# A state times its queries: one full-precision matmul becomes three passes over split operands

## The chip, the cores and the metric

The kernel runs on one core of a Trainium2 chip. The metric is the device time of one execution in microseconds. The engines named below: TensorE (PE, with its weight loads PEld), VectorE (DVE), ScalarE (ACT), GpSimd (POOL), and SyncE (SP), whose queue issues the DMAs.

## The reference, cut to what matters

The program is one layer of an encoder: a projection of 2048 tokens, a gated linear recurrence in both directions (8 heads of 128), a neighbourhood attention (16 heads of 64), a gate on each, an output projection and a norm. The change lies in the recurrence. One direction of it, chunk by chunk:

```python
def step(state, xs):
    qc, kc, vc, dc = xs
    o = jnp.einsum('bhtd,bhdv->bhtv', qc, state)
    state = dc[..., None] * state + jnp.einsum('bhtd,bhtv->bhdv', kc, vc)
    return state, o
...
o = direction(zf_fw, lb_fw, False) + direction(zf_bw, lb_bw, True)
o = _rmsnorm(o.transpose(0, 2, 1, 3), norm_g).reshape(B, S, HG_WIDTH)
return o.astype(g_in.dtype) * jax.nn.silu(g_in)
```

The backward direction runs over the tokens from the last to the first. So an output of the first 1024 tokens needs the backward state that the last 1024 tokens leave.

## The kernel before, in words

All work is in float32. Where a product may not lose precision, an operand is split in a high part that fits a shorter format (float32r) and the low rest, and the product is made as three matmuls: high x high, high x low, low x high. The projections (`proj_mm`, line L278, and `vproj`, line L291) are made so. Other products take plain float32 operands in one call, L676 among them; the profile shows such a call as two records.

The recurrence (`hgrn`, `hgrn_tail`) goes over the 8 heads with the first 1024 tokens (first half, `half == 0`), and then over the 8 heads with the last 1024 (second half). A half has two groups of 512 tokens (`g`), a group four blocks of 128. In the first half the backward state that will come in from the second half isn't known yet. So `hgrn_tail` stores for each head and group, in DRAM:

- `op_d`: the output as far as it is known (tile `ob`);
- `sg_d`: the gate;
- `qb_d`: the queries, decayed to the end of the half (tile `qb`, made on VectorE at L663).

In the second half, when the head's backward state `R` (tiles of the tag `Sb`, L647 and L649) is complete, `hgrn_tail` loads these three again (L671 to L673, tiles of the tag `cl`, a ring of three buffers), multiplies `R` with the queries (L676), adds the stored output (L677), and goes through the norm (`rms_out`: the square at L345, its split at L347 and L349, two matmuls with ones at L354 and L355, ScalarE at L357 and L358, VectorE at L359 and L361, the store to `yq` at L362).

`weave` mixes two streams on TensorE: the steps of the recurrence, and the projection for the next head (L278), whose weights come through `load_split` (loads L262 into a ring of four, split on ScalarE at L268 and on VectorE at L269). The tail of one head (`hgrn_tail`) runs inside the next head's steps. TensorE's order is the order in which the code emits; the other engines' and SP's order is set by a scheduler that places each instruction by a simulated time and by priority. Where the recurrence ends and the attention begins, the two phases share memory and are ordered as one list, TensorE's rows too.

The attention's second half begins with copies: `Prep.k` copies keys into `KA` and `KB` on ScalarE (L978), then copies each to the other 64 partitions by DMA (L979), three pieces each; `load_bias` (L732) loads two bias tables; `alone` fills `Z` (L766); the first score matmuls are L1041 and L1046. The last values for the attention are projected meanwhile by `vproj` (L291), emptied from PSUM on ScalarE (L299, tile `vt`) and stored to `nv` (L301).

Two numberings are used: line numbers are those of the kernel before; in the changed kernel everything from L677 on stands eight lines later.

Of the kernel before, what the change touches and what calls it, by code (L numbers as in the profile page):

```python
# [10 lines left out]
F32 = mybir.dt.float32  # L11
F32R = mybir.dt.float32r
U32 = mybir.dt.uint32
AF = mybir.ActivationFunctionType
ALU = mybir.AluOpType
# [4 lines left out]
P = 128  # L20
KT = D // P
HALF = 1024
GRP = 512
NHEAD = 8
# [14 lines left out]
def body(ctx: ExitStack, tc: tile.TileContext, t):  # L39
    nc = tc.nc  # L40
    dve, act, pool, pe = nc.vector, nc.scalar, nc.gpsimd, nc.tensor
    dma = nc.sync.dma_start
    x, out = t["x"], t["out"]
# [9 lines left out]
    @contextmanager  # L53
    def psum_phase(name, psb, pmap={}):
        with tc.tile_pool(name="p" + name, bufs=1, space=PSUM, reuse_waits="tile") as q:
            cur.update(psum=q, ps=psb, map=pmap)
            yield

    @contextmanager
    def phase(name, bufs, smap={}):  # L60
        with tc.tile_pool(name=name, bufs=1, reuse_waits="tile") as p:
            cur.update(pool=p, bufs=bufs, smap=smap)
            yield

    def dram(name, shape, dt=F32):
        if name in t:
            return t[name]
        return nc.dram_tensor(name, shape, dt, kind="Internal").ap()
# [4 lines left out]
    c_d = dram("c_d", (D,))  # L73
    hs = [dram(f"hs{k}", (P, 2, HALF)) for k in range(KT)]
    op_d = [dram(f"op{i}", (P, HALF)) for i in range(NHEAD)]
    qb_d = [dram(f"qb{i}", (P, HALF)) for i in range(NHEAD)]
    sg_d = [dram(f"sgd{i}", (P, HALF)) for i in range(NHEAD)]
    nq_d = [dram(f"nq{i}", (P, 512)) for i in range(NPAIR)]
    nk_d = [dram(f"nk{i}", (P, 768)) for i in range(NPAIR)]
# [8 lines left out]
    def nm(s):  # L88
        cnt[0] += 1
        return f"{s}_{cnt[0]}"  # L90

    def tl(tag, dt=F32, shape=None):
        if tag in cur["smap"]:
            tag = cur["smap"][tag]
            return sh.tile([P, 512], dt, tag=tag, name=nm(tag), bufs=SH[tag])
        return cur["pool"].tile([P, 512] if shape is None else shape, dt, tag=tag, name=nm(tag), bufs=cur["bufs"].get(tag, 1))
# [4 lines left out]
    def ps(tag="mx"):  # L101
        if tag == "pj":
            return pp.tile([P, 512], F32, tag=tag, name=nm("pj"))
        tag = cur["map"].get(tag, tag)
        return cur["psum"].tile([P, 512], F32, tag=tag, name=nm("ps"), bufs=cur["ps"][tag])
# [221 lines left out]
    def hgrn_init():  # L327
        p = cur["pool"]
        msk["mskd"] = p.tile([P, 3, 32], F32, tag="mskd", name="mskd")
        dma(msk["mskd"], t["mskd"])  # L330
        for i in range(2):
            b = p.tile([P, 2 * P], F32, tag=f"pdb{i}", name=f"pdb{i}")
            pool.memset(b, 0.0)
            pdb.append(b)
        for u in range(NHEAD):
            sfb.append(p.tile([P, P], F32, tag=f"sfb{u}", name=f"sfb{u}"))
# [6 lines left out]
    def rms_out(u, g, o_sb, sg, tok, rest=False):  # L343
        sq = tl("t")
        act.activation(sq, o_sb, AF.Square)  # L345
        sh_ = tl("rh", F32R)
        dve.tensor_copy(sh_, sq)  # L347
        sl_ = tl("rl", F32R)
        dve.tensor_tensor(sl_, sq, sh_, op=ALU.subtract)  # L349
        yield  # L350
        if rest:
            yield
        pss = ps("ss")
        pe.matmul(pss, ones, sh_, start=True, stop=False)  # L354
        pe.matmul(pss, ones, sl_, start=False, stop=True)  # L355
        r = tl("t")
        act.activation(r, pss, AF.Ln, scale=1.0 / 128.0, bias=eps_rms)  # L357
        act.activation(r, r, AF.Exp, scale=-0.5)  # L358
        dve.tensor_mul(r, r, o_sb)  # L359
        yv = tl("t")  # L360
        dve.tensor_tensor(yv, r, sg, op=ALU.mult)  # L361
        dma(yT[u][:, tok:tok + 512], yv)  # L362
# [60 lines left out]
    def hgrn(u, half, st, tail):  # L423
# [197 lines left out]
        for _ in tail:  # L621
            pass
        return hgrn_tail(u, half, sgs, ubs, decs, qibs, os_, decb_all)

    HSUM = 54

    def hgrn_tail(u, half, sgs, ubs, decs, qibs, os_, decb_all):

        R = None
        if half == 0:  # L630
            ds_ = tl("dsuf", shape=[P, 8])
            pool.memset(ds_[:, 7:8], 1.0)
            for b in range(6, -1, -1):
                dve.tensor_mul(ds_[:, b:b + 1], ds_[:, b + 1:b + 2], decb_all[:, b + 1:b + 2])
        obs = {}
        for g in (1, 0):
            po = os_[g]
            pend = []
            for b in range(3, -1, -1):
                sl = slice(b * P, (b + 1) * P)  # L640
                if R is not None:
                    pend.append((sl, R))
                if half == 0 and g == 0 and b == 0:
                    break
                rn = tl("Sb", shape=[P, P])
                if R is None:
                    dve.tensor_copy(rn, ubs[g][:, sl])  # L647
                else:
                    dve.scalar_tensor_tensor(rn, R, decs[1, g][:, b:b + 1], ubs[g][:, sl], op0=ALU.mult, op1=ALU.add)  # L649
                R = rn  # L650
            yield
            for sl, r in pend:
                pe.matmul(po[:, sl], r, qibs[1, g][:, sl], start=False, stop=True, skip_group_check=True)
            ob = tl("t")
            act.activation(ob, po, AF.Copy)
            tk = slice(g * 512, (g + 1) * 512)
            if half == 0:
                dma(op_d[u][:, tk], ob)
                dma(sg_d[u][:, tk], sgs[g])
                qb = tl("t")  # L660
                for b in range(4):
                    sl = slice(b * P, (b + 1) * P)
                    dve.tensor_scalar(qb[:, sl], qibs[1, g][:, sl], ds_[:, g * 4 + b:g * 4 + b + 1], 1.0, op0=ALU.mult, op1=ALU.mult)  # L663
                dma(qb_d[u][:, tk], qb)
            else:
                yield from rms_out(u, g, ob, sgs[g], HALF + g * 512, g == 0)
        if half == 1:
            for g in range(2):
                tk = slice(g * 512, (g + 1) * 512)
                qb, o1, sg = tl("cl"), tl("cl"), tl("cl")  # L670
                dma(qb, qb_d[u][:, tk])  # L671
                dma(o1, op_d[u][:, tk])
                dma(sg, sg_d[u][:, tk])  # L673
                yield
                po = ps("pc")
                pe.matmul(po, R, qb, start=True, stop=True)  # L676
                dve.tensor_tensor(o1, po, o1, op=ALU.add)  # L677
                yield from rms_out(u, g, o1, sg, g * 512)

# [494 lines left out]
    SH = {"e": 8, "q": 4, "vt": 4, "gt": 2, "sg": 4, "bk": 4}  # L1174
    HPS = ({"tr": 1, "pu": 1, "pa": 1, "pb": 1, "po": 2}, {"ss": "po", "pc": "po"})
    NPS = {"sc": 2, "pt": 2, "po": 2}
    HB = {"c": 3, "qi0": 1, "qi1": 2, "v": 2, "pm": 1, "ub": 1, "Sf": 5, "Sb": 5, "pd": 1, "dec": 4, "decb": 1, "dsuf": 1, "g": 3, "ei": 1, "de": 2, "ke": 1, "kx": 1, "qx": 1, "x": 4, "t": 2, "cl": 3, "rh": 1, "rl": 1}
    SB_ = {"ada": 4, "x": 16, "nb": 1}
    NB0 = {"V": 6, "pbuf": 4, "pt": 4, "yv": 1, "bias": 3, "x": 8, "s": 3}
    NB1 = {"V": 6, "pbuf": 4, "pt": 4, "bias": 3, "Q": 6}  # L1180
# [275 lines left out]

    with psum_phase("h", *HPS), phase("h", HB, SMH), tc.manual_schedule(engines={mybir.EngineType.PE}):
        hgrn_init()
        tail = iter(())
        for i in range(16):  # L1460
            half, u = divmod(i, 8)
# [136 lines left out]
    with psum_phase("n1", NPS), phase("n1", NB1, SM1), tc.manual_schedule(engines={mybir.EngineType.PE}):  # L1598
# [32 lines left out]
        m, r, c, pts = pipe.pop(0)  # L1631
        m.sums(r, c, pts)
        turn(pipe, 1)
        m, r, c, pts = pipe.pop(0)
# [73 lines left out]
```

## Time and profile before

| | |
|---|---|
| median of 3 runs | 2605.03 us (2604.98 to 2605.67) |
| the profiled execution | 2604.75 us |
| its span, first to last instruction | 2602.9 us |
| granted TensorE clock, mean | 0.995 |
| busy: TensorE / VectorE / ScalarE | 98% / 67% / 55% |
| recurrence, first half's tails | 607 to 1109 us |
| recurrence, second half's L676 | 1204 to 1715 us |
| first score matmul of the attention's second half | 1740.96 us |

A row of the timeline reads: start in us from the span's start, duration in us, engine, line, operation, tile written <- tiles read, shapes, how many in a row, and in brackets the idle time of the engine ahead of it with what ended it. A row of the chain has start, duration and what. A matmul's recorded duration overlaps with the next one's; the distance from start to start is what it takes of the engine's stream.

### The profile page before, as it was taken

How to read it: one execution, taken by the hardware profiler on the slowest of the kernel's cores; microseconds unless marked ns; L12 is line 12 of the kernel's file. 1: busy time of each engine (PE TensorE's matmuls, PEld its weight loads, DVE VectorE, ACT ScalarE, POOL GpSimd, SP SyncE). 2: the span in 40 equal slices, each digit the busy share in tenths (PEclk: the TensorE clock that was granted, in tenths of full speed). 3: DMA queues.
4: the chain of work that ended last, by engine and by line, in shares of the span. 5: the costliest groups of instructions: out<-in, count | busy, mean ns of one | idle time of the engine just before them, and what ended most of it. 6: DMA issues, size and time to landing. Idle time of an engine off the chain costs nothing.

```text
span 2602.9 us, 45883 instructions
## 1 busy us (share of the span) xinstructions
PE 2558.5 (98%) x17180; PEld 2148.5 (83%) x17180; DVE 1740.2 (67%) x4362; ACT 1432.5 (55%) x2853; POOL 109.1 (4%) x143
## 2 busy tenths in 40 slices
PE   8999999999999999999999999999999999999998
PEld 6888788878888888888888888888888887788887
DVE  7445445377777778877788777555777778648443
ACT  5533444376666666666667666455777777531110
POOL 0000000000000000000000000000000000042221
PEclk9999999999999999999999999999999999999999
DMA  7566454212111126212212222344445556444331
GB/s 293 144 206 153 143 179 136 90 50 74 58 65 66 58 78 227 78 49 75 76 63 63 74 74 76 111 136 143 128 136 141 146 133 173 134 152 129 96 97 57
DMA packets 225920, 296.40 MB, mean 114 GB/s; under 512 B 28840, under 2 KB 117544, under 8 KB 224552
## 3 DMA queue, kind: packets, MB, share of 16 engines
q1 hardware_dynamic: 225695, 293.46, 37.1%
q8 instruction: 135, 2.21, 0.4%
q14 instruction: 90, 0.73, 0.1%
HBM read 218.18 MB, written 66.99 MB: 110 GB/s over the span
## 4 chain that ended last, share of the span: by engine, by line
PE 92%; DVE 3%; ACT 2%; DMA 2%; issue 0%; SPq 0%; DVEq 0%; ACTq 0%
PE pj L278 51%; PE pj L291 6%; PE ps L1535 4%; PE ps L1534 4%; PE ps L1533 4%; PE ps L1112 3%; PE ps L1090 3%; PE ps L482 2%; PE ps L474 2%; PE ps L1041 1%; PE ps L549 1%; PE ps L278 1%; PE ps L573 1%; PE ps L521 1%; PE ps L1048 1%; PE ps L575 1%
## 5 line engine op out<-in xcount | busy, mean ns | idle before, releaser
L278 PE MATMUL pj<-h,wh 128*128 128x512 f32 x3984 | 1268.9, 400 | 3.6 <-ACT wh L825 1.9
L278 PEld LDWEIGHTS pj<-h,wh 128*128 128x128 f32 x3984 | 722.5, 188 | 155.3 <-issue 13.8
L278 PE MATMUL pj<-h,wl 128*128 128x512 f32 x1992 | 781.0, 392 | 0.0
L278 PEld LDWEIGHTS pj<-h,wl 128*128 128x128 f32 x1992 | 374.1, 188 | 83.0 <-DVE wl L826 0.4
L1062 ACT ACTIVATE pbuf<-pbuf,mx 128x480 f32<-128x480 f32 (+5 forms) x256 | 152.5, 597 | 110.8 <-DVE mx L1057 109.9
L1057 DVE CUSTOM_DVE_ANT_1 pbuf<-ps,bias 128x480 f32<-128x480 f32 (+5 forms) x256 | 129.2, 540 | 102.7 <-PE ps L1046 43.1
L291 PE MATMUL pj<-wh,h 128*128 128x256 f32 x1024 | 195.7, 286 | 0.3 <-ACT e L774 0.3
L291 PEld LDWEIGHTS pj<-wh,h 128*128 128x128 f32 x1024 | 162.9, 191 | 4.0 <-issue 1.3
L269 DVE TENSOR_TENSOR wl<-wr,wh 128x512 fp32r<-128x512 f32 x192 | 131.3, 685 | 47.6 <-ACT wh L268 46.6
L268 ACT ACTIVATE wh<-wr 128x512 fp32r<-128x512 f32 x192 | 120.1, 626 | 73.6 <-PE pj L278 61.9
L291 PE MATMUL pj<-wl,h 128*128 128x256 f32 x512 | 144.7, 283 | 0.0
L1096 ACT ACTIVATE pt<-ps 120x384 f32<-120x384 f32 (+3 forms) x128 | 65.2, 510 | 118.3 <-PE ps L1090 118.1
L1094 DVE COPY pt<-ps 120x384 f32<-120x384 f32 (+3 forms) x128 | 74.9, 585 | 62.7 <-PE ps L1090 61.6
L1090 PE MATMUL ps<-ident,pbuf 128*128 128x128 f32 (+2 forms) x832 | 112.8, 273 | 4.0 <-DVE pbuf L1067 2.0
L1090 PEld LDWEIGHTS ps<-ident,pbuf 128*128 128x128 f32 (+2 forms) x832 | 96.5, 136 | 22.1 <-ACT pbuf L1062 3.3
L468 DVE TENSOR_TENSOR de<-e,de 128x512 f32<-128x512 f32 x64 | 44.2, 690 | 95.9 <-ACT de L467 94.7
L1509 ACT ACTIVATE yh<-yr 128x512 fp32r<-128x512 f32 x52 | 32.7, 628 | 132.5 <-PE ps L1534 115.6
L1582 DVE TENSOR_TENSOR vt<-ps,gt 128x512 f32<-128x512 f32 x24 | 16.5, 692 | 131.0 <-PE ps L1535 131.0
L1067 DVE TENSOR_SCALAR pbuf<-pbuf,mx 128x480 f32<-128x480 f32 (+5 forms) x256 | 100.9, 412 | 3.8
L774 ACT ACTIVATE e<-pj 128x512 f32<-128x512 f32 x97 | 57.8, 596 | 79.9 <-PE pj L278 73.0
L291 PEld LDWEIGHTS pj<-wl,h 128*128 128x128 f32 x512 | 97.9, 191 | 1.4 <-issue 0.5
L449 DVE TENSOR_TENSOR_SCAN c<-c,g 128x128 f32<-128x128 f32 x256 | 88.5, 405 | 10.7 <-ACT c L439 10.7
(285 smaller groups left out, 4699.2 us busy)
## 6 DMA issues: line engine op xcount, KB each, us to landing
wr<-in_w_in SPq DMA_DIRECT2D x276, 256.0 KB
yr<-yq SPq DMA_DIRECT2D x64, 256.0 KB
bias<-tint SPq DMA_DIRECT2D x24, 480.0 KB
x<-in_x SPq DMA_DIRECT2D x32, 256.0 KB
ada<-in_ada_m SPq DMA_DIRECT2D x8, 1024.0 KB
wr<-in_w_v SPq DMA_DIRECT2D x32, 256.0 KB
nv<-vt SPq DMA_DIRECT2D x32, 256.0 KB
hs<-s SPq DMA_DIRECT2D x32, 256.0 KB
```

The costliest lines, as they stand in the source:

```text
L268: act.activation(hi, raw, AF.Copy)
L269: dve.tensor_tensor(lo, raw, hi, op=ALU.subtract)
L278: pe.matmul(pz, a, b, start=(k == 0 and n == 0), stop=(k == KT - 1 and n == 2))
L291: pe.matmul(pzs[tp][:, i * 256:(i + 1) * 256], a, b, start=(k == 0 and n == 0 and i == 0), stop=(k == KT - 1 and n == 2), skip_group_check ...
L449: dve.tensor_tensor_scan(c[:, sl], c[:, sl], L[:, sl], 0.0, op0=ALU.add, op1=ALU.subtract)
L1057: return dve.tensor_tensor_reduce(s[:, 0:nk].rearrange("p (r c) -> p r c", c=kw), sc[:, 0:nk].rearrange("p (r c) -> p r c", c=kw), bt[:, 0 ...
L1062: act.activation(s[:, 0:nk], s[:, 0:nk], AF.Exp, scale=-1.0, bias=mx[:, 0:1], accum_out=mx[:, 1:2])
L1067: dve.tensor_scalar(s[:, 0:nk], s[:, 0:nk], mx[:, 2:3], 1.0, op0=ALU.mult, op1=ALU.mult)
L1090: pe.transpose(ptp[0:cw, c * P:(c + 1) * P], s[:, c * cw:(c + 1) * cw], ident)
L1533: pe.matmul(pz, yh[:, kk], wh, start=first, stop=False)
L1534: pe.matmul(pz, yh[:, kk], wl, start=False, stop=False)
L1535: pe.matmul(pz, yl[:, kk], wh, start=False, stop=last)
```

## The change

In the first half the decayed queries `qb` are split before they are stored: `qh` on ScalarE, the rest `ql` on VectorE, and both go to DRAM. In the second half `R` is split into `Rh` and `Rl` (two more tiles of the tag `Sb`) on VectorE, both query parts are loaded, and the product is made in three passes. The tag `cl`, now used in both halves, has four buffers instead of three.

```diff
-    qb_d = [dram(f"qb{i}", (P, HALF)) for i in range(NHEAD)]
+    qb_d = [dram(f"qb{i}", (P, 2, HALF)) for i in range(NHEAD)]
...
-                qb = tl("t")
+                qb, qh, ql = tl("t"), tl("cl", F32R), tl("cl", F32R)
                 for b in range(4):
                     sl = slice(b * P, (b + 1) * P)
                     dve.tensor_scalar(qb[:, sl], qibs[1, g][:, sl], ds_[:, g * 4 + b:g * 4 + b + 1], 1.0, op0=ALU.mult, op1=ALU.mult)
-                dma(qb_d[u][:, tk], qb)
+                act.activation(qh, qb, AF.Copy)
+                dve.tensor_tensor(ql, qb, qh, op=ALU.subtract)
+                dma(qb_d[u][:, 0, tk], qh.bitcast(F32))
+                dma(qb_d[u][:, 1, tk], ql.bitcast(F32))
             else:
                 yield from rms_out(u, g, ob, sgs[g], HALF + g * 512, g == 0)
         if half == 1:
+            Rh, Rl = tl("Sb", F32R, [P, P]), tl("Sb", F32R, [P, P])
+            dve.tensor_copy(Rh, R)
+            dve.tensor_tensor(Rl, R, Rh, op=ALU.subtract)
             for g in range(2):
                 tk = slice(g * 512, (g + 1) * 512)
-                qb, o1, sg = tl("cl"), tl("cl"), tl("cl")
-                dma(qb, qb_d[u][:, tk])
+                qh, ql, o1, sg = tl("cl", F32R), tl("cl", F32R), tl("cl"), tl("cl")
+                dma(qh.bitcast(F32), qb_d[u][:, 0, tk])
+                dma(ql.bitcast(F32), qb_d[u][:, 1, tk])
                 dma(o1, op_d[u][:, tk])
                 dma(sg, sg_d[u][:, tk])
                 yield
                 po = ps("pc")
-                pe.matmul(po, R, qb, start=True, stop=True)
+                for i, (a, b) in enumerate(((Rh, qh), (Rh, ql), (Rl, qh))):
+                    pe.matmul(po, a, b, start=i == 0, stop=i == 2)
                 dve.tensor_tensor(o1, po, o1, op=ALU.add)
                 yield from rms_out(u, g, o1, sg, g * 512)
...
-    HB = {"c": 3, "qi0": 1, "qi1": 2, "v": 2, "pm": 1, "ub": 1, "Sf": 5, "Sb": 5, "pd": 1, "dec": 4, "decb": 1, "dsuf": 1, "g": 3, "ei": 1, "de": 2, "ke": 1, "kx": 1, "qx": 1, "x": 4, "t": 2, "cl": 3, "rh": 1, "rl": 1}
+    HB = {"c": 3, "qi0": 1, "qi1": 2, "v": 2, "pm": 1, "ub": 1, "Sf": 5, "Sb": 5, "pd": 1, "dec": 4, "decb": 1, "dsuf": 1, "g": 3, "ei": 1, "de": 2, "ke": 1, "kx": 1, "qx": 1, "x": 4, "t": 2, "cl": 4, "rh": 1, "rl": 1}
```

On TensorE the rows of the recurrence stay in their order, and each L676 becomes three rows (L684). ScalarE and VectorE get one more row in each of the 16 places of the first half; VectorE gets two more per head in the second. Rows change places in one stretch, where the recurrence ends. There TensorE's first matmul with ones of the last head's last norm (L354) stood before as follows (`pj` is the PSUM tile of the value projection, `wh` and `wl` its split weights, `h` the tokens, the numbers tell tiles apart):

```order
L291 MATMUL pj_18523<-wh_18357,h_10802 128x256
L291 MATMUL pj_18523<-wl_18358,h_10802 128x256
L291 MATMUL pj_18523<-wh_18357,h_10804 128x256
L354 MATMUL ps_18660<-rh_18626,ones 128x512
L291 MATMUL pj_18766<-wh_18744,h_10355 128x256
L291 MATMUL pj_18766<-wl_18745,h_10355 128x256
```

The same place on TensorE now:

```order
L291 MATMUL pj_18693<-wh_18521,h_10864 128x256
L291 MATMUL pj_18942<-wh_18920,h_10415 128x256
L291 MATMUL pj_18942<-wl_18921,h_10415 128x256
L291 MATMUL pj_18942<-wh_18920,h_10417 128x256
L354 MATMUL ps_18836<-rh_18802,ones 128x512
L291 MATMUL pj_18942<-wh_18920,h_10415 128x256
```

L354 moved behind the first three matmuls of the next value tile. That tile takes one of two PSUM buffers that ScalarE's L299 empties. Between L354 and the second matmul with ones, L355, stood 11 rows of L291; now there are 20.

On SP's queue, behind the last head's last store to `yq`, stood two bias loads, the six key copies and two stores of values; in brackets what each row waits for (each DMA takes the next of eight completion semaphores, DMAHW0 to 7, and waits until the DMA that had it before has landed):

```order
L732 DMA bias_18721<-tint 128x1x960 [waits DMAHW7_49,DMAHW6_49,DMAHW5_49]
L732 DMA bias_18723<-tint 128x1x960
L979 DMA KA_3551_18689<-KA_3551_18689 64x512 [waits DMAHW0_49,Activation_49]
L979 DMA KB_3552_18690<-KB_3552_18690 64x512 [waits DMAHW1_49,Activation_49]
L979 DMA KA_3551_18689<-KA_3551_18689 64x256 [waits DMAHW2_49,Activation_49]
L979 DMA KB_3552_18690<-KB_3552_18690 64x256 [waits DMAHW3_49,Activation_49]
L979 DMA KA_3551_18689<-KA_3551_18689 64x256 [waits DMAHW4_49,Activation_49]
L979 DMA KB_3552_18690<-KB_3552_18690 64x256 [waits Activation_49]
L301 DMA nv<-vt_18864 128x2x256 [waits DMAHW6_49,Activation_49]
L301 DMA nv<-vt_18867 128x2x256 [waits DMAHW7_49,Activation_49]
```

SP's queue there now:

```order
L740 DMA bias_18897<-tint 128x1x960 [waits DMAHW7_49,DMAHW6_49,DMAHW5_49]
L740 DMA bias_18899<-tint 128x1x960
L987 DMA KA_3615_18865<-KA_3615_18865 64x512 [waits DMAHW0_49,Activation_49]
L987 DMA KB_3616_18866<-KB_3616_18866 64x512 [waits DMAHW1_49,Activation_49]
L987 DMA KA_3615_18865<-KA_3615_18865 64x256 [waits DMAHW2_49,Activation_49]
L987 DMA KB_3616_18866<-KB_3616_18866 64x256 [waits DMAHW3_49,Activation_49]
L987 DMA KA_3615_18865<-KA_3615_18865 64x256 [waits DMAHW4_49,Activation_49]
L301 DMA nv<-vt_19040 128x2x256 [waits Activation_49]
L301 DMA nv<-vt_19043 128x2x256 [waits DMAHW6_49,Activation_49]
L987 DMA KB_3616_18866<-KB_3616_18866 64x256 [waits DMAHW7_49]
```

The sixth key copy, the third of KB, moved behind the two stores of values, and it now waits for the semaphore that the second bias load had.

## The prediction

> **What bounds the kernel now.** I read the page first: the busy times (part 1) and the chain that ended last (part 4).
>
> ```profile
> PE 2558.5 (98%) x17180; PEld 2148.5 (83%) x17180; DVE 1740.2 (67%) x4362; ACT 1432.5 (55%) x2853; POOL 109.1 (4%) x143
> ...
> PE 92%; DVE 3%; ACT 2%; DMA 2%; issue 0%; SPq 0%; DVEq 0%; ACTq 0%
> ```
>
> TensorE is busy 98% of the span and holds 92% of the chain. So a change is worth what it takes from or adds to TensorE's stream, plus any wait that it makes or removes there. The waits of TensorE in the second recurrence half and the start of the attention after it (1150 to 1800 us) are few; the two that matter here (who waited for whom: us in total, times, longest):
>
> ```profile
> PE ps L1041 <- DMA KA<-KA: 3.2, 1, 3.2
> ...
> PE ps L354 <- DVE rh L347: 0.8, 1, 0.8
> ```
>
> The longest of the first half (540 to 1150 us), total, times and longest in us as above:
>
> ```profile
> PE ps L482 <- ACT ke L476: 3.0, 2, 2.2
> ```
>
> The changed matmul is L676. By its own line it has 32 records, two for each of its 16 matmuls. The chain from 1640 to 1670 us shows what a pair costs in the stream (start, us, what):
>
> ```profile
> L676 PE MATMUL ps<-cl,Sb x32: 590/592/595, 1204.3 to 1715.3; 128*128 128x512 f32 x32
> ```
>
> ```profile
> 1651.73 0.86 PE ps L676 x2
> 1652.59 5.49 PE pj L278 x24
> ```
>
> The records overlap, so the recorded 592 ns is not the price; the distance to the next matmul is. One full-precision L676 takes 0.86 us of the stream. A split 128x512 matmul (L278) takes 5.49 / 24 = 0.229 us.
>
> **The matmul.** Three split passes take 3 x 0.229 = 0.686 us in place of 0.86: 0.174 us saved, 16 times, 2.8 us. The bounds: if the passes didn't overlap, each would cost its mean record, 0.392 us (the page's L278 group with wl), or 1.18 us, which is 0.32 x 16 = 5.1 us lost; at best they cost 0.215 each (0.86 / 4), 3.4 us saved. I take 0.229, because L278 has the same shape and operand kind and the passes stand among L278 matmuls.
>
> ```profile
> L278 PE MATMUL pj<-h,wl 128*128 128x512 f32 x1992 | 781.0, 392 | 0.0
> ```
>
> **First half: the split of the queries.** Per head and group there is one more 128x512 copy on ScalarE (as L268), one more 128x512 subtraction on VectorE (as L269) and one more 256 KB store: 16 of each.
>
> ```profile
> L269 DVE TENSOR_TENSOR wl<-wr,wh 128x512 fp32r<-128x512 f32 x192 | 131.3, 685 | 47.6 <-ACT wh L268 46.6
> L268 ACT ACTIVATE wh<-wr 128x512 fp32r<-128x512 f32 x192 | 120.1, 626 | 73.6 <-PE pj L278 61.9
> ```
>
> That is 10.0 us on ScalarE and 11.0 us on VectorE, none on TensorE. What hides it is the idle time of both engines just after the place. In the second head's tail (686 to 693 us) the rows stand so:
>
> ```profile
> 687.34 0.59 ACT L379 ACTIVATE e<-pj 128x512 f32<-128x512 f32 x1
> 689.96 0.60 ACT L476 ACTIVATE ke<-ps 128x512 f32<-128x512 f32 x1 [2.03 <-PE ps L474]
> ...
> 688.16 0.42 DVE L435 TENSOR_SCALAR e<-e 128x512 f32<-128x512 f32 x1
> 689.46 0.29 DVE L495 COPY Sf<-ps 128x128 f32<-128x128 f32 x1 [0.88 <-PE ps L482]
> ...
> 692.47 1.06 PE L482 MATMUL ps<-v,ke 128*128 128x128 f32 x8
> ```
>
> The copy goes in just ahead of L379, the subtraction just ahead of L435. ScalarE then waits 2.03 us for TensorE's L474, VectorE 0.88 us for its L482. Both gaps are longer than the inserted 0.63 and 0.69 us, and TensorE ends both, so nothing moves behind them. L476 ends at 690.56 and L482 reads it at 692.47: 1.9 us to spare if the cover should be gone. Cost: 0 (bounds: 0, and 0.3 us x 16 = 4.8 us if half of each ScalarE copy shows on TensorE).
>
> The stores go through SP's queue, where the second one of each group waits for the subtraction. Behind it stand weight loads into four buffers that are used tens of microseconds later. SP issues in a third of a microsecond, and a 256 KB store takes about 2 us:
>
> ```profile
> 1700.31 2.01 DMA yq<-t
> ```
>
> Head 0's loads for the second half were issued early in the first half; now their ring is in use, so they stand at its end, behind the last head's stores:
>
> ```profile
> 1108.74 1.03 SPq L664 DMA_DIRECT2D qb<-t  x1
> ```
>
> Their matmul comes at 1204 us, over 90 us later. Cost 0.
>
> **Second half: the split of the state, and the loads.** Two 128x128 VectorE operations per head, eight heads. The nearest rows are 0.35 us (L649, 348 ns) for the subtraction and 0.28 us (L647, 285 ns) for the cast; 0.6 us per head.
>
> ```profile
> L649 DVE SCALAR_TENSOR_TENSOR Sb<-Sb,dec,ub 128x128 f32<-128x128 f32 x32 | 11.1, 348 | 4.3 <-PE ps L653 2.9
> L647 DVE COPY Sb<-ps 128x128 f32<-128x128 f32 x8 | 2.3, 285 | 1.1 <-PE ps L482 1.1
> ```
>
> They are due some 20 us ahead of the matmul. The tight spot is the second norm (L354, L355). For the first head (1203 to 1221 us):
>
> ```profile
> 1216.50 0.69 DVE L677 TENSOR_TENSOR cl<-ps,cl 128x512 f32<-128x512 f32 x1 [2.72 <-DMA cl<-op]
> 1219.65 0.69 DVE L349 TENSOR_TENSOR rl<-t,rh 128x512 fp32r<-128x512 f32 x1
> ...
> 1216.79 0.60 ACT L476 ACTIVATE ke<-ps 128x512 f32<-128x512 f32 x1 [4.46 <-PE ps L474]
> 1217.29 1.27 ACT L467 ACTIVATE de<-c 128x128 f32<-128x128 f32 x4
> 1218.46 0.62 ACT L345 ACTIVATE t<-cl 128x512 f32<-128x512 f32 x1
> ...
> 1220.40 0.50 PE L355 MATMUL ps<-rl,ones 128*128 128x512 f32 x1
> ```
>
> L349 ends at 1220.34, 0.06 us ahead of L355. But what holds it is ScalarE: L345 stands behind L476 and L467, and L476 waits for TensorE's L474, which follows the changed matmul and comes earlier with it. L677 is done at 1217.19, 1.27 us ahead of L345; the 0.35 us that TensorE gains here fit in. The extra load of each group adds 0.33 us of issue on SP at a place where SP is idle for microseconds, and its data is due many microseconds later. Cost 0; so heads 0 to 6 save 14 x 0.174 = 2.4 us.
>
> **Where half of it is lost: the way into the attention.** Here the change moves rows. The chain from 1700 to 1745 us:
>
> ```profile
> 1714.28 3.30 DMA cl<-op
> ...
> 1719.55 0.51 PE ps L354
> 1720.06 1.30 PE pj L291 x11
> 1721.35 0.24 PE ps L355
> 1721.62 0.70 ACT t L357
> ...
> 1730.39 10.44 DMA KA<-KA
> 1740.82 0.14 issue
> 1740.96 0.73 PE ps L1041 x2
> ```
>
> The last head's norm waits for L354 and L355; its store lets the bias loads go, which stand in SP's queue ahead of the key copies (KA, KB), and TensorE waits 3.2 us for the third KA. In the new order L354 stands three L291 matmuls later, and L355 has 20 of them behind L354 instead of 11. Those three need a buffer that ScalarE's L299 must empty first:
>
> ```profile
> 1718.94 1.07 ACT L299 ACTIVATE vt<-pj 128x512 f32<-128x512 f32 x2
> ```
>
> Half of that pair is over at about 1719.5, so TensorE resumes at 1719.4 or so instead of 1719.55, and the 0.35 us of the last head go into this wait. From there it is L354 (0.23) and 23 L291 (1.30 / 11 = 0.118 each, 2.7 us) to L355, at 1722.3; before, 0.23 + 1.30 led to 1721.1. The norm, the store and the bias loads come 1.2 us later, the third KA lands 1.2 us later, and TensorE waits that much longer. What is late next: the third KB. It now stands behind two stores of nv and waits for the second bias load:
>
> ```profile
> 1730.99 0.59 SPq L979 DMA_DIRECT2D KB<-KB  x1
> 1734.46 4.14 SPq L301 DMA_DIRECT2D nv<-vt  x2
> ```
>
> The two nv stores of this row waited for the two bias loads; the second was issued at 1738.23 (the row's end, 1738.60, less one issue), so bias 2 had landed by then. With the 1.2 us, KB goes at 1739.4 instead of 1730.99. With the store's 2.0 us or the op load's 3.3 us it lands at 1741.4 to 1742.7; the second L1041 wants it at 1741.29 + 1.2 = 1742.5. I call it even, 0 to 0.2 us.
>
> The sum: -2.4 + 1.2 = -1.2 us. The profiled execution took 2604.75 us (span 2602.9), 0.28 under the median of 2605.03. So: span 2601.7, and a median of **2603.8 us**.
>
> [...] Does the late KB sit behind the bias loads? DMA packets in three stretches (1729 to 1731, 1731 to 1735, 1738 to 1741 us):
>
> ```profile
> DMA packets 178, 0.39 MB, mean 193 GB/s; under 512 B 24, under 2 KB 56, under 8 KB 178
> DMA packets 247, 0.56 MB, mean 139 GB/s; under 512 B 32, under 2 KB 128, under 8 KB 247
> DMA packets 652, 0.58 MB, mean 194 GB/s; under 512 B 60, under 2 KB 648, under 8 KB 650
> ```
>
> The four 64-partition copies of 1 KB rows need 256 packets. 32 + 96 = 128 of them ran by 1735, while bias packets (2 to 8 KB) still ran; the third KA landed only at 1740.8. So one of the two directions got through early and the other sat behind the bias. [...]
>
> **Rivals.**
> (a) The whole gain arrives: the later L355 costs nothing, since the wait on KA hangs on the bias loads alone. For it: KA took 10.44 us from its issue. Against: the bias loads themselves wait for the norm's store. 2605.0 - 2.8 = 2602.2 us.
> (b) Slower: the third KB takes what the third KA took, 10.4 us, because its direction is the slow one or nv's 512 KB go first. From its issue at 1739.4 that is 1749.8 instead of 1742.5: +7.3 us, 2611 us. It decides from a landing 4.5 us after the issue on; with nv's 512 KB ahead at 166 GB/s (between the 139 and 194 of the rows above), 3.1 us, it would be 2607 us.
> (c) Stalls in the heads: 0.3 us in each of 16 groups because the added ScalarE and VectorE work has no cover after all: 2603.8 + 4.8 = 2608.6 us. Against: the gaps above.
> (d) The passes don't overlap: 2605.0 + 5.1 + 1.2 = 2611 us. Against: 3984 L278 of this shape do.
>
> **How the numbers follow.** Forecast 0.55, (a) 0.2, (b) 0.13, (c) 0.08, (d) 0.04. A measurement of this kernel tells 0.2% (5.2 us) from no change; forecast and (a) lie within it, as do (c) and the milder end of (b). Over +5.2 us: half of (b), (d), a tail of (c): 0.11. Below -5.2 us nothing of these reaches; 0.04 for what I don't see. Range: 2601.5, under (a) by the pass's lower bound, to 2608.0, which takes in the milder (b) and most of (c).
>
> **What would show it.** In the changed profile: three records per matmul on its line, 0.69 us apart to the next; no new waits of TensorE before 1690 us, and everything there some 2.4 us earlier by the last head; L355 1.2 us later against its surroundings; a wait of TensorE before the first scores matmul of the attention of 4 to 5 us instead of 3.2, on KA or on KB. The prediction is wrong if that wait is above 8 us, if L354 waits in every head, or if the distance behind the three passes is near 1.2 us.

## The result and the profile after

The changed kernel took 2608.52 us (median of 22 runs), the kernel before 2604.64 us (22 runs on the same chip). The ratio is 1.0013, with a 95% interval from 1.0008 to 1.0019: slower by 3.4 us (2 to 5). The forecast was 2603.8, 1.2 us faster, with a range of 2601.5 to 2608.0. Of all the executions below one is left out: a single run of 5125.52 us, of the kernel before with its key copies moved, about twice as long as the ten others of that kernel.

TensorE is still what bounds the kernel. From the page of the changed kernel, the busy times:

```profile
PE 2559.0 (98%) x17196; PEld 2153.7 (83%) x17196; DVE 1753.8 (67%) x4394; ACT 1441.6 (55%) x2869; POOL 108.7 (4%) x143
```

VectorE has 13.6 us more work and ScalarE 9.1 us, near the 15.8 (11.0 and eight times 0.6) and 10.0 us of the working. The changed matmul (now L684), by its line and in the chain (start, us, what):

```profile
L684 PE MATMUL ps<-cl,Sb x48: 389/394/478, 1205.7 to 1713.9; 128*128 128x512 f32 x48
```

```profile
1651.19 0.70 PE ps L684 x3
```

Three records each, 0.70 us of the stream where one took 0.86. TensorE's waits in the first half (total, times, longest) are those of before on L476, and a little more on kx:

```profile
PE ps L482 <- ACT ke L476: 3.0, 2, 2.2
PE ps L521 <- DVE kx L512: 1.4, 1, 1.4
```

In the second half and at the start of the attention (1150 to 1800 us) the list has changed:

```profile
PE ps L1049 <- DMA V<-nv: 3.7, 1, 3.7
PE pj L291 <- ACT vt L299: 2.0, 2, 1.9
...
PE ps L1049 <- DMA KB<-KB: 0.9, 1, 0.9
```

The first row is the wait for the third KA (the view names a later DMA); it was 3.2 us before. The wait on L299 is new, that on KB too, and L354's 0.8 us are gone. All new waits of these lie between 1716 and 1745 us. The chain there:

```profile
1712.23 0.70 DVE t L359
1712.95 4.10 DMA cl<-op
...
1717.13 0.70 DVE cl L685
...
1718.40 0.59 ACT vt L299
...
1719.03 0.62 PE pj L291 x3
1719.65 0.24 PE ps L354
1719.89 3.88 PE pj L291 x20
1723.77 0.24 PE ps L355
...
1729.59 10.67 DMA bias<-tint
1740.28 3.82 DMA KB<-KB
...
1744.23 0.64 PE ps L1049
```

Three things are to be seen. The load of op goes the moment that L359 of the group before ends (1712.93). The 20 rows of L291 took 3.88 us, where 20 x 0.118 are 2.4. And the third KB was issued at 1740.28, 10.7 us behind the bias loads that it waits for.

Why L299 was late can be read on ScalarE. There it stands behind L345, which waits for L685 and so for the load of op:

```profile
1717.86 0.63 ACT L345 ACTIVATE t<-cl 128x512 f32<-128x512 f32 x1 [3.59 <-DVE cl L685]
1718.40 1.07 ACT L299 ACTIVATE vt<-pj 128x512 f32<-128x512 f32 x2
```

In the kernel before, L299 stood behind L345 too (it started at 1718.94 us), but no row of TensorE ahead of L354 needed the buffer that it empties. In the new order three rows do, so the late load of op now stops TensorE as well.

Matmul by matmul against before, the changed kernel is 1.6 us ahead behind the last L684 (the first L291 row with `wl` after it starts at 1714.24 instead of 1715.83 us) and 4.2 us behind at 1747 us. So this stretch of some 35 us costs 5.8 us in the profiled execution, and the recurrence ahead of it gains. (The 1.6 us are not 2.8 because this execution was 1.5 us behind at 1204 us already, ahead of the first changed matmul; the section on the hardware says from what. Of the 4.2 us, 2.1 come back between 2150 and 2240 us, far behind the change; why was not followed.)

### The profile page after: what moved, and what is told of

Its sections match the earlier page's. It is cut to its first block, busy times and chain, and to the rows that moved or that the text cites. A ratio compares the mean times of both kernels' runs of the same rounds, so it can differ in the third digit from the quotient of the medians.

```text
span 2605.1 us, 46028 instructions
## 1 busy us (share of the span) xinstructions
PE 2559.0 (98%) x17196; PEld 2153.7 (83%) x17196; DVE 1753.8 (67%) x4394; ACT 1441.6 (55%) x2869; POOL 108.7 (4%) x143
## 4 chain that ended last, share of the span: by engine, by line
PE 92%; DVE 3%; DMA 3%; ACT 1%; issue 0%; SPq 0%; DVEq 0%; ACTq 0%
PE pj L278 52%; PE pj L291 6%; PE ps L1541 4%; PE ps L1543 4%; PE ps L1542 4%; PE ps L1120 3%; PE ps L1098 3%; PE ps L482 2%; PE ps L474 2%; PE ps L1049 2%; PE ps L549 1%; PE ps L278 1%; PE ps L573 1%; PE ps L1056 1%; PE ps L521 1%; PE ps L575 1%
## 5 line engine op out<-in xcount | busy, mean ns | idle before, releaser
L291 PE MATMUL pj<-wh,h 128*128 128x256 f32 x1024 | 197.6, 287 | 2.3 <-ACT vt L299 2.0
L291 PEld LDWEIGHTS pj<-wh,h 128*128 128x128 f32 x1024 | 165.0, 193 | 6.1 <-ACT vt L299 3.4
L291 PE MATMUL pj<-wl,h 128*128 128x256 f32 x512 | 145.8, 285 | 0.0
L291 PEld LDWEIGHTS pj<-wl,h 128*128 128x128 f32 x512 | 99.1, 194 | 1.0
```

Of the source, the lines that this page charges most:

```text
L291: pe.matmul(pzs[tp][:, i * 256:(i + 1) * 256], a, b, start=(k == 0 and n == 0 and i == 0), stop=(k == KT - 1 and n == 2), skip_group_check ...
```

## The experiments

The theory after this comparison: the passes gain what they should, the added work is covered, and the loss sits where the recurrence meets the attention. The rival: the added ScalarE, VectorE and DMA work costs something in every head (rival (c) of the prediction). Later runs split the loss itself. Times are medians, and each ratio is against the kernel before on the same chip; kernels with added lines show other line numbers.

**The last head alone, and all but the last.**

```diff
+                if u == 7:      # second kernel: u < 7
                     act.activation(qh, qb, AF.Copy)
...
-                for i, (a, b) in enumerate(((Rh, qh), (Rh, ql), (Rl, qh))):
-                    pe.matmul(po, a, b, start=i == 0, stop=i == 2)
+                if u == 7:
+                    for i, (a, b) in enumerate(((Rh, qh), (Rh, ql), (Rl, qh))):
+                        pe.matmul(po, a, b, start=i == 0, stop=i == 2)
+                else:
+                    pe.matmul(po, R, qb, start=True, stop=True)
```

> Only the last of the eight heads (u = 7) has the split queries and the three passes; the other seven keep the full-precision matmul. The whole computation is done. Theory 1 (the loss sits on the way into the attention): here stands the whole loss and almost none of the gain. Matmuls save 2 x 0.174 = 0.35 us; the wait of TensorE before the first scores matmuls, 3.2 us before, becomes 4.5 to 6, the second norm's last matmul (L355 of before) comes behind 20 L291 rows, and with half-clock stretches of 3.4 us behind the waits (1.7 us each) the time is 4 to 6 us above before. Rival (the added ScalarE, VectorE and DMA work in all heads costs the time): one head of eight, at most 0.6 us above before.

> Heads 0 to 6 have the split queries and the three passes, the last head keeps the full-precision matmul and one load. The whole computation is done. Theory 1: the gain of 14 x 0.174 = 2.4 us without the loss at the boundary: 2.4 us under before (2 to 3), the wait before the first scores matmul stays near 3.2 us. Rival (the added work in the heads costs the time): 7/8 of the loss is still there, 3 to 4 us above before.

With the last head alone: 2610.39 against 2605.19 us, ratio 1.0018 (1.0009 to 1.0027), 4.7 us slower. One head of eight brings all of the loss. The waits of 1150 to 1800 us have the new kinds, nearly as long (3.4 and 0.9 us ahead of the first scores matmuls, 4.5 to 6 expected):

```profile
PE ps L1062 <- DMA KA<-KA: 3.4, 1, 3.4
PE pj L291 <- ACT vt L299: 1.2, 2, 1.1
...
PE ps L1062 <- DMA KB<-KB: 0.9, 1, 0.9
```

All but the last: 2601.46 against 2605.19 us, ratio 0.9986 (0.9977 to 0.9995), 3.6 us faster (1.3 to 6.0), where 2.4 was expected of the matmuls. In its profile TensorE gains 2.5 us on before between 1204 and 1712 us, as the 14 passes should, and another 2.3 us from there to 1760 us. The waits tell where those came from; the 3.2 us ahead of the first scores matmul did not stay as expected:

```profile
PE ps L1062 <- DMA KA<-KA: 1.2, 1, 1.2
...
PE ps L1062 <- DMA KB<-KB: 0.6, 1, 0.6
```

The rival falls. But the second kernel has a better boundary than the kernel before, though its last head is as before. What differs there is the ring of four buffers.

**The first half's split alone.** The split and its stores (into a tensor that nothing reads) are added to the kernel before, with four buffers.

```diff
+                act.activation(qh, qb, AF.Copy)
+                dve.tensor_tensor(ql, qb, qh, op=ALU.subtract)
+                dma(qs_d[u][:, 0, tk], qh.bitcast(F32))
+                dma(qs_d[u][:, 1, tk], ql.bitcast(F32))
                 dma(qb_d[u][:, tk], qb)
```

> The kernel before, with the first half's split of the queries added (copy, subtraction, two more stores per group, into tensors that nothing reads) and four buffers; the second half is as before. The whole computation is done. Theory 1: the added 10 us of ScalarE and 11 us of VectorE work are covered: within 0.5 us of before. Rival (no cover): up to 0.3 us in each of 16 groups, 2 to 5 us above before, and waits of TensorE on L476 or L435 work that before does not have.

2604.64 against 2605.19 us, ratio 0.9996 (0.9988 to 1.0005): no cost that can be told. The ScalarE rows of the place that the prediction showed (lines stand one later than before, so L380 is its L379, L477 its L476):

```profile
686.55 0.63 ACT L665 ACTIVATE cl<-t 128x512 fp32r<-128x512 f32 x1
687.07 0.59 ACT L380 ACTIVATE e<-pj 128x512 f32<-128x512 f32 x1
689.17 0.60 ACT L477 ACTIVATE ke<-ps 128x512 f32<-128x512 f32 x1 [1.51 <-PE ps L475]
```

The wait on TensorE is 1.51 us instead of 2.03: the copy has gone into it. Since the ring is larger here too, the fair partner is the kernel before with four buffers (below; ratio 0.9990, and the two intervals overlap). TensorE's rows keep the same distance in these two executions, 0.04 us, from 600 to 1700 us, over all 16 splits. The changed kernel itself shows the same: it is 1.50 us behind before at 600 us and at 1200 us.

**The ring.** The kernel before with four buffers instead of three; and the changed kernel with five instead of four.

```diff
-    "cl": 3,
+    "cl": 4,
```

> The kernel before with a fourth buffer in the ring of the recurrence's loads (cl), nothing else; the whole computation is done. Theory 2 (what decides is the ring's size against the tiles of a group: with as many buffers as tiles the load of op takes the buffer of the last group's op, which comes free late; with one more it takes that of the queries, free right after the matmul): the last op load stands ahead of the norm's store of the group before, L354 and L355 are 7 rows apart, TensorE's wait before the first scores matmuls falls from 3.2 to about 1.9 us, and the time is 1.3 us under before (0.5 to 2.5). Rival (only the matmul passes change the time): within 0.5 us of before.

> The changed kernel with a ring of five buffers in place of four; the whole computation is done. Theory 2: the whole gain of the passes, 16 x 0.174 = 2.8 us, and the 1.3 us of the earlier op load: 4.1 us under before (3 to 5.5), with no wait of TensorE on L299 at about 1718 us, the third KB ahead of the two nv stores, and 1.9 us of waiting before the first scores matmuls. Rival (the passes of the last head, or its extra load, bring the loss whatever the ring): 3 us above before, as with four buffers.

The kernel before with four buffers: 2602.87 against 2606.80 us, ratio 0.9990 (0.9981 to 0.9999), 2.6 us faster (0.3 to 5.0), more than the 1.3 expected; its wait before the first scores matmuls fell to 0.9 us, not to 1.9. The changed kernel with five: 2600.09 us, ratio 0.9976 (0.9967 to 0.9985), 6.3 us faster (3.9 to 8.6). There the wait on L299 is gone, as expected; the wait before the first scores matmuls was 2.8 us rather than 1.9, in a profiled execution (2605.83 us) that was the slowest of its 11. SP's queue in the changed kernel, with four buffers and then with five (start, us to issue, what):

```profile
1712.95 0.33 SPq L679 DMA_DIRECT2D cl<-op  x1
1713.67 0.33 SPq L362 DMA_DIRECT2D yq<-t  x1
...
1726.88 0.33 SPq L362 DMA_DIRECT2D yq<-t  x1
1728.89 1.30 SPq L740 DMA_DIRECT2D bias<-tint  x2
...
1733.42 3.35 SPq L301 DMA_DIRECT2D nv<-vt  x2
1740.28 0.47 SPq L987 DMA_DIRECT2D KB<-KB  x1
```

```profile
1707.87 0.40 SPq L679 DMA_DIRECT2D cl<-op  x1
...
1721.41 0.33 SPq L362 DMA_DIRECT2D yq<-t  x1
1723.46 1.31 SPq L740 DMA_DIRECT2D bias<-tint  x2
...
1727.94 0.59 SPq L987 DMA_DIRECT2D KB<-KB  x1
1731.39 4.26 SPq L301 DMA_DIRECT2D nv<-vt  x2
```

A group takes four tiles of the ring in the changed kernel (two of queries, op, gate). With four buffers op takes that of the last group's op, which L359 reads last; with five it takes that of ql, free once the passes are done. So op is loaded 5.1 us earlier. With that the scheduler's order changes too: L355 stands 7 rows behind L354 (12 in the kernel before, 21 in the changed one), the last store to yq goes 5.5 us earlier, and the third KB stands ahead of the nv stores. The gain of five buffers was larger than the 3 to 5.5 us expected, but its interval reaches down to 3.9 us. The run doesn't tell the earlier load from the order that comes with it.

In the kernel before, three buffers and three tiles made the same late load, only milder: op was loaded at 1714.28 us, right behind L359, and with the fourth buffer at 1707.86:

```profile
1707.86 0.33 SPq L672 DMA_DIRECT2D cl<-op  x1
```

**The queue.** The six key copies stand ahead of the first bias loads in SP's queue: in the changed kernel (four buffers, and five) and in the kernel before.

```diff
-                dma(z[y, o].bitcast(F32), z[x, o].bitcast(F32))
+                (pinned if self.first else lambda x: x)(dma(z[y, o].bitcast(F32), z[x, o].bitcast(F32)))
...
-            dma(bf, table_ap(tint[p], 22, jt, 8, 0, 15))
+            (pinned if p == 0 else lambda x: x)(dma(bf, table_ap(tint[p], 22, jt, 8, 0, 15)))
```

> The changed kernel with its four buffers, and only the key copies ahead of the first bias loads in SP's queue; the third KB still stands behind the two nv stores. The whole computation is done. If the loss is the late keys (wait of 3.7 and 0.9 us and the half clock behind them): these waits fall under 1 us, the wait on L299 of 1.9 us stays with the half clock behind it, and the time is 1 to 4 us under before. Rival (the loss is the late op load itself, or the third KB stays late behind nv): 1 to 3 us above before.

> The changed kernel with five buffers, and in SP's queue the six copies of the keys (KA, KB) ahead of the first bias loads; the whole computation is done. If the wait before the first scores matmuls hangs on the bias loads ahead of the copies: the wait (1.9 us with five buffers) is gone, and the time is 5 to 6.5 us under before. Rival (the bias loads are then late themselves, or the copies take as long without them): no better than five buffers alone, 3 to 4 us under before, with a wait on bias in place of that on the keys.

> The kernel before, with the six copies of the keys ahead of the first bias loads in SP's queue; the whole computation is done. If the wait of 3.2 us before the first scores matmul hangs on the bias loads: the third KA lands 3 us or more earlier, the wait is under 1 us, and the time is 2 to 3 us under before. Rival (the copies themselves take 10 us): the wait stays above 2.5 us, the time within 0.5 us of before.

Changed kernel, four buffers: 2603.09 against 2605.24 us, ratio 0.9992 (0.9983 to 1.0000), 2.1 us faster than before (0 to 4.4), where without the move it was 3.4 us slower. The waits on KA and KB are gone, and of the new ones that on L299 is what is left:

```profile
PE pj L291 <- ACT vt L299: 2.2, 2, 2.1
```

The third KB still stands behind the nv stores there, and nobody waits for it, since the nv stores no longer wait for bias loads (two loads of V moved ahead of the copies as well):

```profile
1733.09 1.51 SPq L301 DMA_DIRECT2D nv<-vt  x2
1734.65 0.47 SPq L987 DMA_DIRECT2D KB<-KB  x1
1735.17 2.47 SPq L740 DMA_DIRECT2D bias<-tint  x2
```

Its place was not the price; its wait for the bias load's semaphore was. The kernel before with the copies ahead: 2604.08 (median of ten runs) against 2606.80 us, ratio 0.9990 (0.9981 to 0.9999), 2.6 us faster (0.3 to 5.0), as expected; its wait of 3.2 us is gone. With five buffers and the copies ahead the changed kernel took 2598.23 us (six runs), ratio 0.9971 (0.9960 to 0.9983): 7.6 us faster than the kernel before (4.4 to 10.4; 5 to 6.5 were expected), and so faster than both kernels of this case. No wait on bias took the place of that on the keys.

**Half clock.** In this part of the changed kernel TensorE ran at half clock for 3.4 us behind two of its waits. The stretches below are cut where the clock records change (start:end, length, TensorE busy with its records, granted clock, share of DMA, GB/s):

```profile
1716.34:1719.75 3.41, 1.54 (x12) 1.00 0.53 165
1719.75:1723.16 3.41, 3.41 (x18) 0.50 0.72 222
...
1740.23:1743.65 3.42, 0.41 (x1) 1.00 0.39 125
1743.65:1747.06 3.41, 2.83 (x12) 0.50 0.34 90
```

The first of them is why the 20 rows of L291 took 3.88 us; where the clock stayed whole, with the last head alone changed, the same 20 rows took 2.39. To see whether the idle TensorE brings them, matmuls whose result is overwritten went into the second gap:

```diff
+            if self.st.first and R == 1 and j == 0:
+                for _ in range(20):
+                    pe.matmul(scs[0][:, 0:P], ident, ident, start=True, stop=True, skip_group_check=True)
```

> The changed kernel, with 20 matmuls of 128x128 on the identity ahead of the first scores matmul of the attention, in the gap where TensorE waits for the key copies; their result is overwritten. The whole computation is done. If the stretch of 3.4 us at half clock behind that gap (1743.65 us in the changed kernel's profile) comes from the idle TensorE: it is gone, the granted clock from 1743 to 1749 us is 1.00, and the time is 1.5 to 2 us under the changed kernel. Rival (the half-clock stretch falls there by chance, or is set off by the load that follows): it is as often there as before, and the time equals the changed kernel's to 0.5 us.

The same stretches of that kernel, both gaps:

```profile
1717.99:1721.40 3.41, 1.41 (x11) 1.00 0.40 121
1721.40:1724.81 3.41, 3.41 (x18) 0.50 0.71 218
1741.88:1745.29 3.41, 3.41 (x31) 1.00 0.45 146
1745.29:1748.71 3.42, 3.42 (x30) 1.00 0.46 137
```

Behind the filled gap the clock is 1.00; behind the one left open it is 0.50 again. The time, 2607.41 against 2605.19 us (ratio 1.0008, 0.9999 to 1.0017), is 1.3 us better against before than the changed kernel's ratio (1.5 to 2 were expected), but the two intervals overlap: the trace shows it, the time alone does not.

A second try went to another wait, that on L476 at 546 us. Behind it the half clock stood in the kernel before (548.03 us, 6.83 us long), in the changed one (552.39 us, 3.41 us) and with five buffers and the copies ahead (549.87 us, 6.82 us); nine matmuls fill the wait.

```diff
+            if u + half + g == 0:
+                pf = ps("pa")
+                for _ in range(9):
+                    pe.matmul(pf[:, 0:P], ident, ident, start=True, stop=True, skip_group_check=True)
             pu = updates(ke1, v)
```

> The kernel before, with nine full-precision 128x128 matmuls on the identity, about 2 us, in TensorE's wait of 2.2 us on L476 at 546 us; nothing reads their result. The whole computation is done. In every profile so far a stretch of 3.4 or 6.8 us at half clock follows that wait. If the idle TensorE brings it: no such stretch between 546 and 556 us, and the time is 1.5 to 2.5 us under before (half the rate over the part of 3.4 to 6.8 us that TensorE works and isn't kept by VectorE's kx). Rival (the half clock has another cause, or what is saved goes into the next wait): within 0.5 us of before.

> The changed kernel with five buffers, the key copies ahead of the bias loads, and the same nine matmuls in the wait on L476. The whole computation is done, and nothing reads what the nine write. The kernel with five buffers and the copies ahead was 7.6 us under before; if the half clock behind the wait on L476 is gone, 9 to 10 us under before. Rival (the nine save nothing): 7 to 8 us under before.

Neither gain came. In the kernel before: 2606.04 against 2605.24 us, ratio 1.0001 (0.9992 to 1.0011). With the five buffers and the copies ahead: 2598.21 us, ratio 0.9973 (0.9962 to 0.9983), as without the nine. In both TensorE now waits 1.5 us for kx (0.8 in the kernel before, 0.6 with five buffers and the copies ahead, in the same view). In the first of the two the clock drops one stretch later, at 551.61 instead of 548.03 us:

```profile
PE ps L521 <- DVE kx L512: 1.5, 1, 1.5
```

```profile
548.20:551.61 3.41, 1.77 (x43) 1.00 0.23 74
551.61:555.02 3.41, 3.41 (x56) 0.50 0.00 0
```

So part of what TensorE gains in front of kx is waited away behind it. The profiled execution of the second, 2593.07 us, was the fastest of its eight and had the highest mean granted clock, 0.998 (the others 0.995 to 0.997); the median shows no gain. Why is open.

## Why the prediction was wrong

- **The matmul: right.** 0.70 us for three passes, 0.686 forecast. Rival (d) is out. (The lower bound of 0.215 us a pass, 0.86 divided by four, was the author's estimate; no run shows the four.)
- **First half's split and stores at 0: right.** The split alone showed no cost, in time or in TensorE's rows, and the gap named as its cover shrank by 0.52 us. Rival (c) is out.
- **Second half's loads and state split at 0: right in heads 0 to 6.** No new wait of TensorE stands ahead of 1716 us. From behind the first passes (1205 us) to ahead of the last (1712 us) TensorE went from 1.35 us behind the execution of before to 1.4 us ahead: 2.7 us over 14 passes, 2.4 forecast.
- **"Where half of it is lost": wrong, and this is the step that failed.** The change of order was seen, and its price was put at +1.2 us; it was 5.8 us in the profiled execution. By the steps of the working:
  - "Half of that pair is over at about 1719.5, so TensorE resumes at 1719.4 or so", with the last head's 0.35 us gone: the op load took 4.10 us instead of 3.30, L299 stood behind it on ScalarE, TensorE waited 1.87 us on L299 where before it waited 0.81 on L354, and was 1.1 us later. Why the load took longer was not settled; with the last head alone changed it took 3.3 us.
  - "23 L291 (1.30 / 11 = 0.118 each, 2.7 us) to L355": the stretch at half clock adds 1.5 us (3.88 us for 20 rows, 2.39 at full clock). Nothing in the working could have changed the rate of TensorE.
  - "The third KA lands 1.2 us later": the wait for KA grew by 0.5 us, from 3.21 to 3.74.
  - "I call it even, 0 to 0.2 us" for the third KB: it was issued at 1740.28 rather than 1739.4, landed 3.82 us later, at 1744.10, and cost another 1.0 us. The forecast lateness of 1.2 us upstream had become 2.6, and the call was even only at 1.2.
  - Not in the sum: the second stretch at half clock, 1.2 us (from the start of the score matmul on KB to the ninth L291 behind it 2.75 us, before 1.53).
  - 1.1 + 1.5 + 0.5 + 1.0 + 1.2 = 5.3 us, against 5.8 between the two points; 0.4 of the rest is lost around a short second wait on L299 at 1733.85 us. This is the account of one execution. Its two half-clock stretches need not come in each: with the last head alone changed the first one is missing, behind a wait of 1.09 us.
- **The signs named beforehand did not tell.** The wait before the first scores matmuls was to be 4 to 5 us, and it was 3.74 and 0.95, 4.7 in all; none of the signs of being wrong came. They looked at the waits and at the heads. 3.8 of the 5.8 us were in the rate of TensorE (1.5 and 1.2) and in the wait on L299 (1.1), which no sign covered.
- **Rival (b), a late third KB, was the right place** and its time of 2607 to 2611 us holds 2608.5, but with another mechanism: not the copy itself is slow, it is issued late. It had 0.13.
- **Does the late KB sit behind the bias loads?** Its issue did: SP sent it at 1740.28 us, when the second bias load had landed (1729.59 + 10.67 us). From there the copy took 3.82 us in the changed kernel, and with the same place behind nv but no bias ahead (issued at 1734.65 us) nobody waited.
- **Rival (a), the whole gain,** came true once the op load was early, and more than it: with five buffers the kernel was 6.3 us (3.9 to 8.6) under before, where (a) had 2.8. The kernel before had a late op load of its own, worth 2.6 us.

What the working should have asked is why the last op load was late at all. The row "1714.28 3.30 DMA cl<-op" was quoted as part of the chain, and the ring's size stood in the diff. But the fourth buffer was read as room, not as four buffers for four tiles, which keeps the late load just as three for three did.

## What to carry to other kernels

When a ring grows along with the tiles that one turn takes, nothing has become earlier: here the last load of op still waited for the last reader of the same tile of the turn before (L359 ended at 1712.93 us, op was issued at 1712.95; in the kernel before 1714.25 and 1714.28). One buffer more than the tiles can be worth more than the change itself: here it turned 3.4 us slower into 6.3 us faster. A lateness of 1 us in front of a queue (here the store, the bias loads, the key copies, one behind the other) has to be followed to its end, and "even" in such a chain is a call to widen the range upward. On TensorE the two waits of this case, 1.9 and 4.7 us, cost a further 1.5 and 1.2 us in the clock, so a wait can be dearer than its length.

## What the hardware showed that was not expected

In the profiles of the two kernels the starts of the stretches at half clock differ by whole multiples of 3.413 us. Counted from the first (at 12.14 us in the kernel before, 13.09 us in the changed one), the others come 157, 646 and 757 such steps later in the one, and 75, 158, 500, 507 and 758 in the other. A stretch lasted 3.413 or 6.827 us, the one at the very end 8.96 us before and 6.70 us after.

Cut at these steps, from 20 to 2580 us, the traces show how long TensorE was idle (no matmul in the trace) in the step ahead of each stretch:

| kernel | step from, us | idle, us | next step |
|---|---|---|---|
| before | 544.62 | 2.19 | half clock |
| before | 2213.74 | 2.72 | half clock |
| after | 265.68 | 1.91 | half clock |
| after | 548.98 | 2.20 | half clock |
| after | 1716.34 | 1.87 | half clock |
| after | 1740.23 | 3.01 | half clock |
| before | 264.73 | 1.90 | full clock |
| before | 2186.43 | 1.80 | full clock |

The last two rows are the longest idle times that full clock followed. With the nine matmuls in the kernel before, 1.64 us of idle (548.20 us, above) were followed by half clock, so the idle time of a step does not settle it in these runs. The same wait may cost nothing more than itself here, or a stretch at half clock too: by estimate up to 1.7 us for each 3.41 us (half of them; 1.5 and 1.2 us were found above), by where the steps cut it. The kernel before shows the first at the very place of this case (columns as above):

```profile
1735.87:1739.28 3.41, 1.88 (x16) 1.00 0.58 155
1739.28:1742.69 3.41, 1.73 (x11) 1.00 0.45 145
1742.69:1746.11 3.42, 3.42 (x31) 1.00 0.44 127
```

Its wait of 3.2 us is cut by the steps into 1.5 and 1.7 us, and the clock stays at 1.00. A stretch of the same kind is also why the changed kernel's execution was 1.5 us behind the other ahead of the first changed matmul: it had one at 269.09 us that the other had not, and its distance grew there from 0.45 to 1.9 us. How much of the spread of single runs comes from the clock is not shown: of the kernel before, runs of 2601.79 and of 2609.70 us on one chip have the same mean granted clock, 0.995.
